# Two-layer diffusion backbone: the Fourier heads move beside attention, the context's groups move up to the latent weights, the DFT is folded twice

## The chip, the cores and the metric

One core of a Trainium2 chip runs the whole program: two layers, one launch. The metric is the device time of a run in microseconds, as the median of several runs. The shown times of the kernel before are 2538.61, 2540.79 and 2540.26 us, median 2540.26 us.

## What is computed

`x` (1024 latent tokens of width 1024) and `ctx` (256 context tokens) pass two layers; `c` and `c_ctx` give each stream its modulation vectors. Cut to what matters (all in fp32):

```
for i in 0, 1:
    sh1, sc1, g1, sh2, sc2, g2 = split(silu(c) @ ada_w[i] + ada_b[i], 6)        # the same for c_ctx
    hx = rms_norm(x) * norm1_g * (1 + sc1) + sh1;  hc likewise from ctx
    px = hx @ w_in[i]        # columns: Fourier 256, pooling 256, queries 512, keys 256, values 256
    q, k = rope(head_norm(...));  context keys and values from hc, without rope
    ax = softmax(q @ [k, kc].T / sqrt(128)) @ [v, vc]       # 4 query heads, 2 key heads, 1280 keys
    fo = real(fft2(px_fourier as 4 heads of 64, over tokens and features)) @ w_fourier[i]
    po = (windowed means - px_pool) @ w_pool[i] * pool_scale[i]
    x  = x + g1 * (concat(fo, po, ax) @ w_out[i])
    x  = x + g2 * experts(modulated norm of x)              # 16 experts, each takes its 128 tokens
    if i == 0: ctx goes the same way, attending to context keys alone
```

## The kernel before, in words

Everything is one program in Python that writes out the instructions of five engines. fp32 products are made of three fp32r products (`mm3`, line 253: high by high, low by high, high by low), so every operand is split once into a high and a low part (`split`, line 249: a ScalarE copy and a VectorE subtraction). Transposes and some small products are plain fp32.

Buffers come from rings: 43 pages of 128x1024 fp32, 8 halves (512), 4 quarters (256). A page that is taken waits for whoever used that slot last. PSUM has 8 banks; `lone` (line 1525, 1533) keeps single banks to 4 to 7 once attention begins, so that pairs are left for score rows.

The order of the work is written out with generators. `run` takes one to its end, `some(g, n)` takes n steps of it, and `interleave((g, n), ...)` takes steps of several in proportion to the numbers beside them. The scheduler that turns this into one queue per engine may move an instruction a little, but largely keeps that order. SyncE issues the plain loads, in its own order.

A layer's first half, from line 1470 on:

- The latent rows are loaded, normed and modulated (`Normed`, line 405), the Fourier columns projected (`fp_group` with weights `wf`), then the queries (`q_group`, `wq`), the pooling columns (`fp_group`, `wp`), then keys and values (`kv_group`, `wkv`), one step for each 128 tokens. A key step's norm and rope run over ScalarE, VectorE and GpSimd; `turn` transposes 512 tokens of keys at once.
- Beside the latent keys the context rows are loaded and modulated (`context_in`, line 1481). Then `fourier_w` (line 677) multiplies the Fourier weights with the DFT of the features, and the context keys follow.
- Layer 0, line 1526 on: `fourier_x` in proportion 13 to 16 with `context_groups` (line 1511), which loads 1024 columns of the input weights a second time, splits them and makes the context's queries and its Fourier and pooling columns. Then latent pooling (`pool_mix`, line 823) beside the context's Fourier heads (`fourier_c`, line 778), then the context's pooling beside the first 6 score rows.
- Layer 1: `fourier_x` beside the context keys and pooling, then pooling beside the first 6 score rows.
- Attention (line 869) has two generators: `scores`, 32 rows (4 heads x 8 tiles: 6 products of 512 columns and 3 of 256, two row maxima, two exponentials), and `values`, 80 steps (transpose four tiles of weights, split them, 3 products of 512). Line 1543: 60 value steps, 24 rows, and 24 steps of modulation: in layer 0 `ada_part` (line 308), fp32 products with two loaded pages a step; in layer 1 `ada_rows` (line 338), VectorE passes.

`fourier_x` (line 694) before: rows 1 to 511 and 1023 to 513 are added (cosine) or subtracted (sine), products with the feature DFT give U and V of 512 rows; row 512 goes on its own, with one-row products and an alternating sign; then for each of cosine and sine a 512x512 table is loaded and split in two pages, and two output blocks take 12 products of 512 columns each. Four PSUM banks are held until sums and differences give tokens 0 to 511 and 1023 to 513.

```
    DVE.tensor_tensor(out=e[:, 1:512], in0=F[b][:, 1:512], in1=F[b][:, 1023:512:-1],
                      op=OP.subtract if z else OP.add)
```

## Time and profile before

| | |
|---|---|
| median of 3 runs | 2540.26 us (2538.61 to 2540.79) |
| the profiled execution, time | 2545.91 us |
| its span, first to last instruction | 2544.0 us |
| mean granted TensorE clock | 0.981 |
| layer 0: projections / mixed stage / first score rows / rest of attention | 57.0 to 185.2 / 259.7 / 283.5 / 444.0 us |
| layer 1: mixed stage / first score rows / rest of attention | 1592.0 to 1634.8 / 1659.8 / 1808.0 us |

A view by windows gives, for each stretch, how long each engine was busy in it; a view of groups gives the mean duration of one kind of instruction; a view of waits says which engine a queue waited for. All instructions carry line 107, that of the helper that issues them, so a stage is known by the names of its tiles: `pg`, `hf`, `qt` are pages, halves and quarters, `banks` is PSUM, `cs` the constants with the identity (transposes), `altr` the alternating sign, `cond` the condition vector, `mx` the row maxima. The stages' borders in the table are the first products of each kind.

### The profile page before, as it was taken

To read this page: it belongs to the slowest core of one execution; us is meant where nothing else is said; L and a number is where in the kernel's file an instruction comes from. 1 tells how busy PE (TensorE), PEld (TensorE's weight loads), DVE (VectorE), ACT (ScalarE), POOL (GpSimd) and SP (SyncE) were. 2 spreads that over 40 slices of the span, in tenths; PEclk is the share of its full clock that TensorE was granted. 3 is DMA by queue.
4 is the path that set the end of the run, shared out by engine and by line. 5 is a ranking of instruction groups with operands and counts; after the bars stand their busy time and mean duration, and the time that the engine had idled before them with its cause. 6 is when DMAs were issued, how large, how long until landed. Compare 5 with 4: busy or idle time off the path is not lost. (4 is left out here: it accounts for less than half of the span.)

```text
span 2544.0 us, 39662 instructions
## 1 busy us (share of the span) xinstructions
PE 2425.6 (95%) x14709; PEld 1843.9 (72%) x14709; DVE 1930.5 (76%) x3114; ACT 1384.2 (54%) x1934; POOL 324.5 (13%) x350
## 2 busy tenths in 40 slices
PE   7999999999899999999999899899995999999998
PEld 4878667775677777777777687678774778888886
DVE  4547756756988787787777675887746999999997
ACT  4124546422555656666666412466523777787775
POOL 1320000001111011121010252100000111011100
PEclk9999999999999999999999999999997999999999
DMA  7113341547798889899887642210566999999993
GB/s 288 51 33 111 108 133 36 182 143 265 274 285 295 280 281 304 286 289 301 290 291 249 201 149 71 63 42 1 199 223 224 355 345 364 390 382 386 383 398 98
DMA packets 175075, 575.51 MB, mean 226 GB/s; under 512 B 22361, under 2 KB 35065, under 8 KB 174881
## 3 DMA queue, kind: packets, MB, share of 16 engines
q1 hardware_dynamic: 162784, 535.22, 59.0%
q0 software_dynamic: 12096, 37.75, 6.3%
q8 instruction: 115, 1.88, 0.3%
q14 instruction: 80, 0.65, 0.1%
HBM read 535.10 MB, written 37.80 MB: 225 GB/s over the span
## 5 line engine op out<-in xcount | busy, mean ns | idle before, releaser
L107 PE MATMUL banks<-pg,pg 128*128 128x512 f32 (+2 forms) x9656 | 1982.2, 393 | 18.4 <-DVE pg L107 9.9
L107 PEld LDWEIGHTS banks<-pg,pg 128*128 128x128 f32 (+1 forms) x9656 | 1448.4, 172 | 397.1 <-issue 29.8
L107 ACT ACTIVATE pg<-pg 128x1024 fp32r<-128x1024 f32 (+3 forms) x945 | 931.8, 1008 | 550.8 <-PE banks L107 354.3
L107 DVE TENSOR_TENSOR pg<-pg,pg 128x1024 fp32r<-128x1024 f32 (+3 forms) x918 | 1040.9, 1158 | 194.6 <-ACT pg L107 181.6
L107 ACT ACTIVATE pg<-banks 128x512 fp32r<-128x512 f32 (+3 forms) x438 | 243.6, 581 | 242.6 <-PE banks L107 231.3
L107 DVE TENSOR_TENSOR pg<-banks,pg 128x512 fp32r<-128x512 f32 (+2 forms) x404 | 257.6, 662 | 69.0 <-ACT pg L107 64.4
L107 PE MATMUL banks<-cs,pg 128*128 128x128 f32 x1616 | 243.2, 282 | 41.3 <-DVE pg L107 31.5
L107 PEld LDWEIGHTS banks<-cs,pg 128*128 128x128 f32 x1616 | 196.6, 145 | 95.0 <-DVE pg L107 44.6
L107 ACT ACTIVATE hf<-banks 128x512 f32<-128x512 f32 (+3 forms) x126 | 66.4, 541 | 245.9 <-PE banks L107 230.6
L107 PE MATMUL banks<-pg,hf 128*128 128x512 f32 (+1 forms) x660 | 165.2, 371 | 13.8 <-ACT pg L107 6.6
L107 PEld LDWEIGHTS banks<-pg,hf 128*128 128x128 f32 x660 | 113.8, 196 | 48.5 <-ACT pg L107 10.9
L107 DVE TENSOR_REDUCE mx<-banks 128x1 f32<-128x256 f32 (+1 forms) x136 | 106.4, 795 | 33.2 <-PE banks L107 32.4
L107 ACT ACTIVATE pg<-banks,nb 128x256 f32<-128x256 f32 (+1 forms) x136 | 104.2, 773 | 43.4 <-DVE nb L107 40.5
L107 POOL TENSOR_SCALAR rnv<-ss 128x1 f32<-128x1 f32 x38 | 17.5, 461 | 673.6 <-ACT pg L107 610.1
L107 POOL DMA_INDIRECT pg<-xtab,idxx x32 | 45.2, 1414 | 420.9 <-PE banks L107 137.5
L107 POOL DMA_INDIRECT xmid<-pg,idxx x16 | 37.0, 2311 | 448.4 <-DVE pg L107 448.4
L107 DVE TENSOR_TENSOR hf<-banks,pg 128x512 f32<-128x512 f32 x36 | 24.8, 690 | 67.4 <-PE banks L107 67.2
L107 POOL DMA_INDIRECT out_dram<-pg,idxx x16 | 39.7, 2484 | 243.9 <-DVE pg L107 116.1
L107 DVE TENSOR_TENSOR pg<-pg,hf 128x512 f32<-128x512 f32 (+1 forms) x68 | 42.5, 627 | 24.5 <-POOL hf L107 23.5
L107 PE MATMUL banks<-pg,qt 128*32 128x256 f32 x1024 | 58.6, 381 | 0.5 <-ACT qt L107 0.5
L107 PE MATMUL banks<-pg,cond 128*32 128x512 f32 x256 | 56.0, 618 | 2.1 <-DMA pg<-in_ada_w_dram 2.1
L107 PEld LDWEIGHTS banks<-pg,qt 128*32 128x32 f32 x1024 | 31.6, 110 | 25.4 <-issue 2.9
(148 smaller groups left out, 1071.5 us busy)
## 6 DMA issues: line engine op xcount, KB each, us to landing
pg<-in_w_gate_dram SPq DMA_DIRECT2D x256, 512.0 KB
pg<-in_w_up_dram SPq DMA_DIRECT2D x256, 512.0 KB
pg<-in_w_down_dram SPq DMA_DIRECT2D x256, 512.0 KB
pg<-in_ada_w_dram SPq DMA_DIRECT2D x96, 512.0 KB
pg<-in_w_in_dram SPq DMA_DIRECT2D x32, 512.0 KB
pg<-in_x_dram SPq DMA_DIRECT2D x16, 512.0 KB
pg<-in_w_out_dram SPq DMA_DIRECT2D x16, 512.0 KB
xtab<-pg SPq DMA_DIRECT2D x16, 512.0 KB
```

Source lines behind the costliest of these rows:

```text
L107: r = fn(*a, **k)
```

## The change

- `fourier_x` folds the rows a second time, about row 256, into even and odd output tokens; a table becomes one page for each parity (256 columns), row 256 and row 0 or 512 change their places, and the sum for token 512 comes out of the same bank. One bank is held at a time. Even and odd tokens are written with a stride of two.
- In layer 0 the context's loads and modulation start beside the last Fourier columns of the latents, and the context's groups are made with `wf`, `wq` and `wp` as these are in place; `context_groups` and its loads go.
- In layer 0 the context keys come before the latent keys, and latent pooling runs beside the last four latent key steps. In layer 1 two of the four pooling steps run beside the context keys.
- Attention comes straight after. One queue of side work, `beside`, holds what is left: (layer 1: two pooling steps), `fourier_x`, then in layer 0 `fourier_c`, the context's pooling and the two `ada_part`, in layer 1 `ada_rows`. 4 of its steps go beside the first 6 score rows, up to 36 beside the next 60 value steps.

```diff
-    dl = np.stack(dft(T, 512, 512, 1.0 / 256))
+    cl, sl = dft(T, 256, 512, 1.0 / 256)
+    dl = np.stack([np.stack([a[:, par::2] for a in (cl, sl)]) for par in range(2)])
...
-    alt512 = altr[:, None, :].to_broadcast([1, 256, 2])
+    alt256 = altr[:, None, :].to_broadcast([1, 128, 2])
...
+    DVE.scalar_tensor_tensor(altm, iota, 0.0, cs[:, 429:430].to_broadcast([128, 128]), op0=OP.is_equal, op1=OP.mult)
...
-            kb = page()
+            kb = page() if big else half()
...
     def fourier_x(F, pcw, oT):
...
-                e = half()
...
+                e, g = page(), half()
                 DVE.tensor_tensor(out=e[:, 1:512], in0=F[b][:, 1:512], in1=F[b][:, 1023:512:-1],
                                   op=OP.subtract if z else OP.add)
...
+                if z == 0:
+                    DVE.tensor_copy(e[:, 0:513:512], F[b][:, 0:513:512])
+                    split(mid(128 * b, 128 * b + 128), e[:, 256:257].to_broadcast([128, 128]))
...
+                for par in range(2):
+                    DVE.tensor_tensor(out=g[:, 256 * par:256 * par + 256], in0=e[:, 0:256], in1=e[:, 512:256:-1],
+                                      op=OP.add if z == par else OP.subtract)
+                split(fold(512 * b, 512 * b + 512), g.ap)
+                drop(e, g)
+                yield
...
-        pq = []
-        for z in range(2):
-            tab = Weights(dl[z], 512, 4)
-            run(tab.load())
+        for par in range(2):
+            raw, tab = page(), Pair(page)
+            SP.dma_start(raw.ap, dl[par])
+            split(tab(0, 1024), raw.ap)
+            drop(raw)
             for m in range(2):
...
+                for n in range(2):
+                    mm3(p, uv(0, n), tab(256 * n, 256 * n + 256), n == 0, par == 1 and n == 1)
+                if par == 0:
+                    v = p.rearrange("p (a b) -> p a b", b=2)
+                    PE.matmul(v, um[0], alt256, start=False, stop=False)
+                    PE.matmul(v, um[1], alt256, start=False, stop=True)
+                for n in range(2):
+                    mm3(q, uv(1, n), tab(512 + 256 * n, 768 + 256 * n), n == 0, par == 1 and n == 1)
+                if par == 0:
+                    for n in range(2):
+                        for part in uv(0, n):
+                            PE.matmul(q[:, 0:128], part, altm, start=False, stop=False)
+                    PE.matmul(q[:, 0:128], um[0], altm[0:1, :], start=False, stop=False)
+                    PE.matmul(q[:, 0:128], um[1], altm[0:1, :], start=False, stop=True)
                 yield
+                qs = quarter()
+                ACT.activation(qs.ap, q, AF.Copy)
+                x, y = oT(m, 0, 512), oT(m, 512, 512)
...
+                    DVE.tensor_sub(x[:, 1:512:2], p, qs.ap)
+                    DVE.tensor_add(y[:, 511:0:-2], p, qs.ap)
+                drop(qs, ps)
...
-        interleave((fx_steps, 2), (some(rows_of, 3), 3))
-        drop(wf)
+        interleave((fx_steps, 2), (some(rows_of, 3), 3) if last else (some(ci, 2), 2))
...
+        if last:
+            drop(wf)
+            interleave((qx, 8), (wp.load(), 4), (some(rows_of, 12), 12))
+        else:
+            interleave((some(qx, 3), 3), (ci, 7))
...
+            run(fp_group(C, hc, wf, FC[0:2]))
+            drop(wf)
+            interleave((qx, 5), (wp.load(), 4))
+            run(q_group(C, hc, wq, qtab[2], QC))
...
         interleave((fp_group(X, hx, wp, FX[2:4]), 4), (wkv.load(), 4), (some(rows_of, 9), 9))
+        if not last:
+            run(fp_group(C, hc, wp, FC[2:4]))
...
+        if last:
+            interleave((some(kvx, 9), 9), (later(ci, 10), 20))
...
+            run(some(kvc, 1))
+            run(kvx)
+            px = pool_x()
+            interleave((kvc, 3), (some(px, 2), 2))
+        else:
...
+            run(some(kvc, 3))
+            run(some(kvx, 1))
+            run(kvc)
+            run(some(kvx, 4))
+            interleave((some(kvx, 4), 4), (pool_x(), 4))
...
+        cw = fourier_w(i)
+        run(kvx)
         sx, vx = attention(X, Q, kx, kc, oX)
...
+        def beside():
+            yield from px
+            yield from fourier_x(FX[0:2], cw, oX)
+            if last:
...
+                yield from rows_of
+                return
+            yield from fourier_c(FC[0:2], cw, oC)
+            yield from pool_mix(C, FC[2:4], pw, oC)
...
+            yield from ada_part(0, 1)
+            yield from ada_part(0, 2)
+        side = beside()
+        interleave((some(sx, 6), 6), (some(side, 4), 4))
...
-        interleave((some(vx, 60), 60), (some(sx, 24), 24), *side)
+        interleave((some(vx, 60), 60), (some(sx, 24), 24), (side, 36))
```

## Rows read from the trace of the kernel before

**Rows 1.** Page, part 1: busy us, share of the span, instructions.

```profile
PE 2425.6 (95%) x14709; PEld 1843.9 (72%) x14709; DVE 1930.5 (76%) x3114; ACT 1384.2 (54%) x1934; POOL 324.5 (13%) x350
```

**Rows 2.** Windows of layer 0: length, busy us by engine, granted clock, DMA share, GB/s.

```profile
57.00:185.20 128.20, 126.00 (x550) 102.33 (x549) 61.24 (x112) 28.43 (x50) 41.26 (x65) 0.99 0.14 42
185.20:259.70 74.50, 69.19 (x438) 60.47 (x436) 60.08 (x119) 35.59 (x63) 8.18 (x25) 0.98 0.34 102
259.70:283.50 23.80, 20.14 (x88) 15.86 (x89) 18.33 (x53) 14.09 (x31) 0.00 (x0) 0.86 0.21 67
283.50:444.00 160.50, 160.33 (x877) 108.89 (x876) 101.75 (x210) 87.89 (x188) 0.00 (x0) 0.99 0.31 100
```

**Rows 3.** Windows of layer 1, the same columns.

```profile
1592.00:1634.80 42.80, 40.50 (x199) 31.54 (x197) 38.42 (x83) 19.43 (x38) 5.35 (x14) 0.96 0.21 61
1634.80:1659.80 25.00, 19.31 (x84) 14.16 (x84) 21.05 (x43) 14.35 (x31) 0.00 (x0) 0.93 0.16 48
1659.80:1808.00 148.20, 146.41 (x844) 118.85 (x843) 121.08 (x242) 104.33 (x216) 0.00 (x0) 1.00 0.16 52
```

**Rows 4.** Waits of TensorE, layer 0, 185.2 to 283.5 us: total us, times, longest.

```profile
PE banks L107 <- DVE hf L107: 5.6, 3, 3.2
```

**Rows 5.** Waits of TensorE, layer 1, 1592 to 1659.8 us.

```profile
PE banks L107 <- DVE pg L107: 2.3, 1, 2.3
```

**Rows 6.** Timeline of TensorE, layer 0: start us, us, instructions merged.

```profile
179.44 5.76 PE L107 MATMUL banks<-pg,pg 128*128 128x512 f32 x24
...
213.16 0.38 PE L107 MATMUL banks<-qt,altr 1*128 1x256 f32 x1
213.47 1.44 PE L107 MATMUL banks<-pg,pg 128*128 128x256 f32 x10
...
232.87 11.69 PE L107 MATMUL banks<-pg,pg 128*128 128x512 f32 x97
```

**Rows 7.** Groups by shape, 185.2 to 259.7 us: count, busy us, mean ns, idle before.

```profile
L107 DVE TENSOR_TENSOR pg<-pg,pg 128x1024 fp32r<-128x1024 f32 x13 | 15.7, 1217 | 5.2 <-ACT pg L107 3.9 <-PE banks L107 1.3
...
L107 DVE SCALAR_TENSOR_TENSOR hf<-pg,cs,pg 64x512 f32<-64x512 f32 x8 | 6.0, 748 | 0.3
...
L107 DVE TENSOR_TENSOR pg<-banks,pg 128x512 fp32r<-128x512 f32 x8 | 5.4, 680 | 0.0
...
L107 DVE TENSOR_TENSOR pg<-pg 64x512 f32<-64x512 f32 x4 | 2.8, 688 | 0.1
...
L107 DVE TENSOR_TENSOR pg<-pg 128x527 f32<-128x527 f32 x4 | 2.7, 700 | 0.0
...
L107 DVE TENSOR_TENSOR pe<-pg,cs 64x8 f32<-64x8 f32 x10 | 1.5, 158 | 0.1
```

**Rows 8.** The same on VectorE, 1592 to 1659.8 us.

```profile
L107 DVE TENSOR_REDUCE mx<-banks 128x1 f32<-128x1024 f32 x8 | 9.7, 1215 | 2.9 <-PE banks L107 2.9
...
L107 DVE SCALAR_TENSOR_TENSOR pg<-pg,cond,pg 128x1024 f32<-128x1024 f32 x3 | 3.8, 1279 | 0.0
...
L107 DVE TENSOR_REDUCE mx<-banks 128x1 f32<-128x256 f32 x6 | 2.5, 416 | 0.5 <-PE banks L107 0.5
...
L107 DVE TENSOR_TENSOR pg<-banks,pg 128x256 fp32r<-128x256 f32 x5 | 2.0, 418 | 0.0
...
L107 DVE TENSOR_SCALAR nb<-mx 128x1 f32<-128x1 f32 x6 | 1.2, 202 | 0.0
...
L107 DVE TENSOR_TENSOR tot<-sums 128x1 f32<-128x1 f32 x5 | 0.8, 156 | 0.4 <-ACT pg L107 0.2
...
L107 DVE TENSOR_TENSOR hf<-pg,hf 128x128 fp32r<-128x128 f32 x2 | 0.6, 284 | 0.0
```

**Rows 9.** DMA issues, 185.2 to 259.7 us: queue, count, KB each.

```profile
pg<-in_w_in_dram SPq DMA_DIRECT2D x8, 512.0 KB
```

**Rows 10.** Timeline of TensorE, modulation products (cond), layer 0.

```profile
285.63 1.06 PE L107 MATMUL banks<-pg,cond 128*32 128x512 f32 x8
...
300.70 1.04 PE L107 MATMUL banks<-pg,cond 128*32 128x512 f32 x2
```

More of the change, by code (lines that the diff above doesn't have):

```diff
@@ L696, in fourier_x @@
         UV = []
+        midb = half(F32R)
+        mid = lambda a, b: (midb[:, a:b], midb[:, 256 + a:256 + b])
         for z in range(2):
@@ L723, in fourier_x @@
         ps = bank()
-        midb = half(F32R)
-        mid = lambda a, b: (midb[:, a:b], midb[:, 256 + a:256 + b])
-        for b in range(2):
-            split(mid(128 * b, 128 * b + 128), F[b][:, 512:513].to_broadcast([128, 128]))
         for b in range(2):
@@ L767, in fourier_x @@
         drop(umid, *UV)
-        for m in range(2):
-            qs = half()
-            ACT.activation(qs.ap, pq[2 + m].ap, AF.Copy)
-            DVE.tensor_sub(oT(m, 0, 512), pq[m].ap, qs.ap)
-            y = oT(m, 512, 512)
-            DVE.tensor_add(y[:, 511:0:-1], pq[m][:, 1:512], qs[:, 1:512])
-            DVE.tensor_copy(y[:, 0:1], y512[:, m:m + 1])
-            drop(qs, pq[m], pq[2 + m])
-            yield
     def fourier_c(F, pcw, oT):
         cw = lambda z, b: pcw(512 * z + 256 * b, 512 * z + 256 * b + 256)
-        fs = Pair(half)
+        fs, uvs = Pair(page), Pair(page)
@@ L1467, in backbone @@
         fx_steps = fp_group(X, hx, wf, FX[0:2])
-        interleave((some(fx_steps, 2), 2), (hx.modulate(1), 10), *side)
-        interleave((fx_steps, 2), (some(rows_of, 3), 3))
-        drop(wf)
-        qtab = rope_tables(i, q_norm_g, "q")
-        Q = []
-        interleave((q_group(X, hx, wq, qtab, Q), 8), (wp.load(), 4), (some(rows_of, 12), 12))
-        drop(wq, *qtab[:2])
-        FX += [page() for _ in range(2)]
-        ktab = rope_tables(i, k_norm_g, "k")
-        interleave((fp_group(X, hx, wp, FX[2:4]), 4), (wkv.load(), 4), (some(rows_of, 9), 9))
-        drop(wp)
-        kx = KV(X)
         def context_in():
```

122 lines of the change are left out of this document (43 added, 79 removed).

## The prediction

> **What bounds the kernel now.** I read the page first: TensorE is busy 95% of the span, VectorE 76% [rows 1]. Most of that is expert work that the change leaves alone, so I read only the stretches in which each layer goes from its projections to the end of the latent attention, in windows cut where the work changes: 57 to 444 us in layer 0 [rows 2], 1592 to 1808 us in layer 1 [rows 3]. In each, the same stages stand behind each other. The projections are TensorE's (126.00 of 128.20 us busy, VectorE 61.24). Then comes a mixed stage: context keys, Fourier heads, pooling, in layer 0 the context's other groups too. Here VectorE is the full engine (60.08 of 74.50, and 38.42 of 42.80 in layer 1), and TensorE waits for it [rows 4, 5]. The first score rows, up to the first value product, stay on VectorE (18.33 of 23.80, 21.05 of 25.00), with the granted clock at 0.86 and 0.93. After that attention is TensorE's: 160.33 of 160.50 and 146.41 of 148.20 busy, at 0.99 and 1.00. A move therefore helps only if it takes VectorE work out of the middle; TensorE work that it puts beside attention is paid in full.
>
> **Prices of one instruction.** 97 products of 256 columns take 11.69 us and 24 of 512 take 5.76 us [rows 6]: without the last one's tail, 0.119 and 0.232 us each. A product with one row as the weights holds TensorE for 0.31 us (from 213.16 to 213.47 us). On VectorE a pass over 1024 columns takes 1.22 us, over 512 0.68 [rows 7], over 256 0.42, over 128 0.28 [rows 8].
>
> **The folded DFT, per layer.** Before: 62 products of 256 columns, 48 of 512, 6 of one row: 7.4+11.1+1.9 = 20.4 us of TensorE. After, read from the diff: 48 for U and V, 6 for the middle row and 48 for the two tables, all of 256 columns, 102 x 0.119 = 12.1; 8 of one row 2.5; 8 with 128 moving columns. No row has that form: half of 0.119 bounds it from below, the 512-column price from above, 0.5 to 1.9 us; I take 0.119, the nearest, 1.0. Sum 15.6, so 4.8 us less. On VectorE each of the four folds gains two 256-column passes (4 x 0.84), and two of four table splits go (2.4): about 1 us more.
>
> The trace halves the time with the columns. The Trainium skill ("TensorE: Matmul & The Clock Gate", Back-to-back issue gap) gives another sustained spacing, 81 ns at 128 columns and 131 ns at 512, so that the columns hardly count; by that, with an estimate of 98 ns at 256 columns, the products other than the one-row ones would save 1.7 us a layer where rows 6 say 5.4. The measured 0.232 us is far from its 131 ns, so the sum goes by the rows.
>
> **Layer 0, context groups with the latent weights.** Eight loads of 512 KB [rows 9] and their eight splits go, 8 x 1.22 us of VectorE, all out of the mixed stage. The query group's 96 products of 256 become 48 of 512: 11.4 to 11.1 us. The context's loads, modulation, query and Fourier and pooling groups move up among the projections, where VectorE is half idle. On SyncE's queue its two loads now pass the rope tables and the pooling weights; the DMA engines are 14% busy in that stretch, so this costs nothing unless the pages are late. On GpSimd the norms of two query tiles come into a queue busy 41.26 of 128.20. The first Fourier weights stay until the context has used them, and I count all 43 pages in use when the latent keys begin, so a page can be late: from 0 to 4.6 us, twice the nearest wait for one page, 2.3 [rows 5]; I take 2. The last latent key step, before at 185.2 us, then ends at 185.2+11.1 (queries)+11.4 (Fourier, pooling)+11.1 (context keys)+0.4 (their transposes)+2 = 221.2 us.
>
> From there VectorE sets the pace, for pooling now lies beside the last latent key steps. Its passes are 8 over the full width of 0.70, 4 of 0.69, 8 of 0.75 and 16 small ones of 0.16 [rows 7]: 17.0 us. Four key steps of five 256-column passes (8.4) and two splits of transposed keys (1.4) make it 26.8, in 4 x 24 x 0.232 = 22.3 us of TensorE's; 4.5 are left over. Behind them stand the last key step 2.1, the Fourier weights 1.4, the last key splits 1.4 and the first query split 0.7: the first score comes 10.1 us later, at 231.3. Six score rows of 2.16 (a maximum over 1024 columns, one over 256, three small ones [rows 8]) are 13.0, two query splits 1.4, the two cosine folds 5.3, two splits of U 1.4: 21.1, so the first value product comes at 252.4, before at 283.5. The rest of attention is TensorE's 160.5 plus what is put beside it: the Fourier products left 12.7, the context's DFT 48 x 0.119 = 5.7, its pooling 0.9; 2 more for changes between kinds of work.
>
> **Modulation, beside what is left.** The 18 steps that make the modulation rows stand behind Fourier in one queue of side work and get about the second half of the first 60 value steps, where they had three quarters. A step takes TensorE 1.06 us; one that comes apart because its second page is late takes 1.04+1.06 [rows 10]. Of the 16 with loads I count 8 apart now; from -8 to +8 us, I take +2. The end is 252.4+160.5+19.3+4 = 436.2 us against 444: **7.8 us less.**
>
> **Layer 1.** No context groups, the same order. From the last key step at 1592.0 VectorE has its rest 2.5, two context key chains 3.4, half the pooling 7.1 and splits of keys, Fourier weights and query 4.3: 17.3 us, TensorE about 16; the first score comes at 1609.3, before at 1634.8. Then six rows and their query splits 14.4, the other half of pooling 9.9, two folds 5.3: 29.6, the first value at 1638.9, before at 1659.8. Then 148.2+15.6+1.5 = 165.3: 1804.2 against 1808, **3.8 us less.** The three modulation passes of 1.28 us that sat among the first score rows [rows 8] go into the middle, where VectorE has 27 us free.
>
> **Sum.** 11.6 us less, if VectorE never pauses in those four stretches (10.1+21.1+17.3+29.6 = 78.1 us). In layer 1's mixed stage it was busy 90%, and waits of its own chain remain, though pooling and folds fill most: I allow 3. That leaves 8.6 us. The profiled execution took 2545.9 us (span 2544.0 and 1.9 around it), 5.6 over the median of 2540.3; by the sum it becomes 2537, and the median **2532 us**. A measurement of this kernel tells about 0.2%, 5 us, from no change.
>
> **Rivals.**
> - *Stalls get filled.* Up to the first value product I left TensorE idle about 6+7 us in layer 0 and 1+16 in layer 1. If Fourier products and the first transposes are placed there, two thirds, 20 us, come back: **2512**. For: beside attention TensorE's queue already mixes five kinds of work with no idle time. Against: each of them waits for a split on the same full VectorE.
> - *The gain is given back.* All eight whole modulation steps come apart, and TensorE pays 6 us beyond the 2 in the sum: **2538**, no change that could be told. For: twice the load rate, with a ring of pages that is nearly full. Against: the DMA share there is only 0.31.
> - *The change doesn't do what it says:* the folded products don't run at half price, and only the reordering is left. The 4.8 us a layer are gone: **2541**. The row of 97 products speaks against it. By the spacing of the Trainium skill ("TensorE: Matmul & The Clock Gate", Back-to-back issue gap) 3.7 us a layer would be gone, 2539.
> - *Slower: VectorE's queue pauses in front of the scores.* What covered its latencies in the mixed stage, Fourier's product chains, now lies behind; pooling and folds stand in its queue ahead of the row maxima, for which every score waits. If it is busy there only as among the first score rows now, 0.8 in the mean [rows 2, 3], the 78.1 us become 97.6, 16.5 more than with my allowance: **2548**. It decides from 90 us on, a share of 0.87, where the whole 11.6 us are gone. For: those rows are the same work. Against: there VectorE lacked work; now it has a backlog.
>
> **How the numbers follow.** The forecast has 0.40 (own range 2521 to 2542: 0.33 faster, 0.07 same), filled stalls 0.24, gain given back 0.10 and unfolded price 0.04 (together 0.01 faster, 0.12 same, 0.01 slower), the pausing queue 0.22, all slower. Faster 0.58, same 0.19, slower 0.23. The range runs from 2506, the filled stalls with the low ends of the unknown costs, to 2551, the pausing queue with late pages.
>
> **What the next profile would show.** Right: one-row and 256-column products lie inside attention; the first value product comes some 31 us earlier in layer 0 and 20 in layer 1; the rest of attention is longer by 23 and 17 us; eight loads of the input weights are gone; VectorE is over 90% busy from the pooling to the first value. Wrong: if the stretch from the last key step to the first value exceeds 31 us in layer 0 or 47 in layer 1 with VectorE idle in it, the queue pauses; if the rest of attention grows by less than the added products, stalls were filled; if layer 0's last key step ends later than 221 us, pages were late. A change in the experts' stages would be outside all of this.

## The result, and the profile after

Four runs of the changed kernel have a median of 2525.35 us (2524.4 to 2526.89), four of the kernel before 2540.53 us (2538.61 to 2545.41). The ratio is 0.9934 with a 95% interval of 0.9919 to 0.9949: 15.2 us faster, which is clear of the 0.2% that can be told from no change, inside the forecast's range and 6.7 us below its 2532.

The first line of the page of the changed kernel answers to [rows 1]: TensorE has 15.8 us less to do, VectorE 7.8, and the span, 2522.4 us, is 21.6 shorter than the one the prediction was made from.

```profile
PE 2409.8 (96%) x14665; PEld 1830.0 (73%) x14665; DVE 1922.7 (76%) x3124; ACT 1374.4 (54%) x1924; POOL 326.6 (13%) x346
```

The windows of layer 0 in the changed kernel answer to [rows 2]; the columns are the same, and the cuts are again the last latent key step, the first score, the first value product and the end of attention.

```profile
57.00:221.20 164.20, 161.77 (x754) 131.96 (x753) 83.20 (x155) 37.22 (x70) 49.72 (x73) 1.00 0.11 33
221.20:234.60 13.40, 7.30 (x24) 4.51 (x23) 10.81 (x26) 4.85 (x11) 4.36 (x7) 0.75 0.00 0
234.60:257.80 23.20, 19.65 (x106) 16.61 (x107) 20.89 (x48) 15.78 (x36) 0.00 (x0) 0.93 0.00 1
257.80:437.30 179.50, 177.92 (x1029) 126.10 (x1027) 118.61 (x263) 98.25 (x208) 0.60 (x5) 1.00 0.34 110
```

The mixed stage of 74.5 us has become 13.4. Most of its TensorE work now stands in the first window, 161.77 busy of 164.20 us, and in the last, 177.92 of 179.50. Attention ends at 437.3 us; before it was 444.0.

The windows of layer 1 in the changed kernel, answering to [rows 3], with one more row ahead of them, the latent key steps (before: 1534.7 to 1592.0 us):

```profile
1523.20:1574.20 51.00, 47.10 (x215) 38.07 (x214) 31.77 (x63) 15.10 (x33) 16.95 (x34) 1.00 0.22 71
1574.20:1598.20 24.00, 18.50 (x81) 14.16 (x79) 21.07 (x49) 8.56 (x17) 5.07 (x10) 0.93 0.07 17
1598.20:1623.50 25.30, 21.60 (x90) 15.62 (x89) 21.91 (x56) 15.81 (x36) 0.00 (x0) 0.87 0.00 0
1623.50:1787.50 164.00, 162.22 (x959) 132.81 (x958) 138.59 (x274) 112.87 (x228) 1.26 (x2) 1.00 0.20 64
```

The last three windows make 213.3 us, before 216.0. And the key steps, which the prediction left as they were, take 51.0 us where they took 57.3.

TensorE's waits in the changed kernel, layer 0, 221.2 to 257.8 us (total us, times, longest), answering to [rows 4]:

```profile
PE banks L111 <- DVE hf L111: 5.6, 1, 5.6
PE banks L111 <- ACT pg L111: 3.4, 2, 3.2
```

The same view of layer 1, 1574.2 to 1623.5 us, answering to [rows 5]:

```profile
PE banks L111 <- DVE pg L111: 3.6, 2, 2.9
PE banks L111 <- DVE hf L111: 3.4, 2, 2.6
PE banks L111 <- ACT pg L111: 2.2, 3, 1.6
```

VectorE is still what TensorE waits for most between keys and values: 5.6 of 9.5 us in layer 0, all of it for the last pooling step's half (hf), and 7.0 of 9.2 in layer 1. TensorE's timeline in the middle of layer 0's attention answers to [rows 6]:

```profile
285.02 0.97 PE L111 MATMUL banks<-pg,pg 128*128 128x256 f32 x6
285.92 0.48 PE L111 MATMUL banks<-altr,qt 1*128 1x256 f32 x2
286.34 0.98 PE L111 MATMUL banks<-pg,pg 128*128 128x256 f32 x6
287.15 0.56 PE L111 MATMUL banks<-altm,pg 128*128 128x128 f32 x4
287.64 0.43 PE L111 MATMUL banks<-altm,qt 1*128 1x128 f32 x2
```

These are the folded Fourier products, inside attention as the change says. The new form, four products of 128 columns, takes 0.49 us to the next one's start, 0.12 each in the mean. Last, the DMA issues of the changed kernel from 57 to 257.8 us, answering to [rows 9]: the input weights are loaded six times in all that time, and not once behind 185.2 us, where eight loads stood.

```profile
pg<-in_w_in_dram SPq DMA_DIRECT2D x6, 512.0 KB
```

### The profile page after: what moved, and what is told of

Its sections match the earlier page's. It is cut to its first block, busy times and chain, and to the rows that moved or that the text cites. A ratio compares the mean times of both kernels' runs of the same rounds, so it can differ in the third digit from the quotient of the medians.

```text
span 2522.4 us, 39523 instructions
## 1 busy us (share of the span) xinstructions
PE 2409.8 (96%) x14665; PEld 1830.0 (73%) x14665; DVE 1922.7 (76%) x3124; ACT 1374.4 (54%) x1924; POOL 326.6 (13%) x346
## 5 line engine op out<-in xcount | busy, mean ns | idle before, releaser
L111 ACT ACTIVATE pg<-pg 128x1024 fp32r<-128x1024 f32 (+3 forms) x935 | 921.1, 1007 | 527.4 <-PE banks L111 350.5
L111 DVE TENSOR_TENSOR pg<-pg,pg 128x1024 fp32r<-128x1024 f32 (+2 forms) x908 | 1027.5, 1157 | 185.1 <-ACT pg L111 172.9
L111 ACT ACTIVATE pg<-banks 128x512 fp32r<-128x512 f32 (+4 forms) x440 | 245.2, 581 | 258.6 <-PE banks L111 246.2
L111 PE MATMUL banks<-cs,pg 128*128 128x128 f32 x1608 | 239.5, 279 | 37.8 <-DVE pg L111 27.6
L111 PEld LDWEIGHTS banks<-cs,pg 128*128 128x128 f32 x1608 | 190.8, 143 | 92.6 <-DVE pg L111 42.5
L111 PE MATMUL banks<-pg,hf 128*128 128x512 f32 (+1 forms) x612 | 153.5, 373 | 7.0 <-ACT pg L111 5.6
L111 PEld LDWEIGHTS banks<-pg,hf 128*128 128x128 f32 x612 | 105.9, 194 | 35.4 <-ACT pg L111 8.7
L111 DVE TENSOR_REDUCE mx<-banks 128x1 f32<-128x1024 f32 (+1 forms) x136 | 105.7, 795 | 24.0 <-PE banks L111 23.1
L111 POOL TENSOR_SCALAR rnv<-ss 128x1 f32<-128x1 f32 x38 | 21.1, 555 | 525.8 <-ACT pg L111 458.4
```

The costliest lines, as they stand in the source:

```text
L111: r = fn(*a, **k)
```

## The experiments

Twelve runs were made, three of them of unchanged kernels. The theory was the prediction's: the gain is VectorE work taken out of the middle, and cheaper Fourier products. The rivals were that the fold alone does it, that the place of the Fourier heads does it, or that a stage outside the two attentions does it. The table has what the traces of all of them show, cut at the starts of products in TensorE's timeline: the end of layer 0's attention (the first product of its output projection), the expert stage of layer 0, which no kernel changes, then in layer 1 the latent key steps (from the first of their 192 products to the last), the stretch from that last product to the first of the output projection (an earlier cut than the end of the windows above), and the span. All in us.

| kernel | layer 0's attention ends | experts | key steps, layer 1 | last key to output, layer 1 | span |
|---|---|---|---|---|---|
| before | 444.6 | 785.6 | 57.1 | 200.1 | 2544.0 |
| c_before (unchanged) | 444.6 | 787.8 | 55.2 | 199.9 | 2542.5 |
| e_fold | 439.7 | 783.2 | 54.1 | 201.8 | 2533.1 |
| e_unfold | 439.1 | 786.5 | 51.5 | 203.0 | 2533.6 |
| e_front | 434.4 | 787.7 | 52.6 | 198.4 | 2526.2 |
| after | 437.3 | 783.6 | 50.6 | 197.2 | 2522.4 |
| c_after (unchanged) | 438.1 | 783.1 | 52.5 | 196.6 | 2524.4 |
| a_same (unchanged) | 438.1 | 785.7 | 51.9 | 196.9 | 2526.6 |
| e_hyb | 434.4 | 786.3 | 52.9 | 196.8 | 2524.0 |
| e_ktab | 437.6 | 783.2 | 53.2 | 196.7 | 2525.1 |
| e_rows | 439.3 | 786.2 | 53.3 | 197.9 | 2530.2 |
| e_pool | 435.6 | 783.4 | 53.3 | 198.8 | 2525.7 |
| b1 | 433.4 | 783.8 | 52.8 | 196.5 | 2521.0 |
| b3 | 434.1 | 783.8 | 64.4 | 189.8 | 2524.6 |

The experts take 783.1 to 787.8 us, and the changed kernel alone has 783.1, 783.6 and 785.7: two spans may differ by some 4 us that no edit made. So the parts are compared stage by stage, and only where they differ by more than unchanged kernels do. Of the 21.6 us between the first and the sixth row's spans, the four columns hold 7.3, 2.0, 6.5 and 2.9; the other 2.9 are spread over the rest of the kernel.

### Both kernels once more

The unchanged kernels, each with a second profile, to see how far a stage repeats.

> The kernel before, unchanged, for a second profile. In the first one TensorE stood 4.2 us in layer 1's latent key steps for a late load of key weights and then ran 7 us at the low clock; with it the key steps took 57.3 us, in the changed kernel 51.0. Theory (an accident of that one execution): the key steps take 50 to 52 us here and the span is 2536 to 2540. Rival (the order of the loads makes the stall, and the change removed it): 56 to 58 us again, and a span of 2543 to 2546.

> The changed kernel, unchanged, for a second profile. Outside the two stretches that the change rewrites, the first profile of it was some 5 us shorter than that of the kernel before (2 in layer 0's experts, 1.5 at the start of layer 1, 1.9 elsewhere). Theory (these differences are execution noise or small shifts of TensorE's clock): they come out otherwise here, by a microsecond or more each. Rival (they belong to the change): the same stages agree within 0.5 us with the first profile.

The kernel before took 2544.36 us (span 2542.5), the changed one 2526.46 (span 2524.4). The end of layer 0's attention repeats within 0.8 us, and so does layer 1's stretch behind the keys. The experts took 783.1 us in c_after, as its rival had it (783.6 in the first profile), but 785.7 in a_same below. Of the stages that the change touches, the key steps of layer 1 vary most: 57.1 and 55.2 before, 50.6 and 52.5 after. The windows of these steps, first in the kernel before:

```profile
1534.70:1592.00 57.30, 50.96 (x213) 40.66 (x212) 29.54 (x60) 14.34 (x31) 16.64 (x33) 0.91 0.20 70
```

The same steps of c_before:

```profile
1535.30:1590.80 55.50, 50.55 (x214) 40.20 (x213) 28.95 (x60) 13.66 (x30) 16.64 (x33) 0.94 0.21 71
```

And of c_after:

```profile
1524.10:1577.00 52.90, 49.88 (x214) 40.39 (x213) 31.85 (x63) 15.21 (x33) 16.94 (x34) 0.94 0.20 69
```

So the length before was no accident of one profile, though c_before lies between its theory's 50 to 52 us and its rival's 56 to 58. A part of the differences is the clock: the same products keep TensorE busy for 50.96 us at 0.91, 50.55 and 49.88 at 0.94, and 47.10 at 1.00 (the changed kernel's row above).

### The fold alone, and everything but the fold

e_fold is the kernel before with the new Fourier function and its tables in the old places (the function itself, as in the change, is left out here):

```diff
-            interleave((fx, 13), (chain(some(context_groups_, 4), kvc, context_groups_), 16))
+            interleave((fx, 15), (chain(some(context_groups_, 4), kvc, context_groups_), 16))
...
-            interleave((fx, 11), (chain(kvc, some(px, 3)), 4))
+            interleave((fx, 13), (chain(kvc, some(px, 3)), 4))
...
-            drop(*FX[0:2])
```

> The kernel before with the twice-folded DFT alone, in the old order. Theory (the mixed stage belongs to VectorE, so TensorE time saved in it is worth nothing there): 2540 plus or minus 3, with TensorE's Fourier products at 15 to 16 us a layer instead of 20 to 25. Rival (the saving of 4.8 us a layer is had wherever it lies): 2531.

e_front is the changed kernel with the Fourier heads of the latents ahead of attention again, so it has the fold and the context groups with the latent weights, but not the Fourier heads beside attention:

```diff
+        run(fourier_x(FX[0:2], cw, oX))
         sx, vx = attention(X, Q, kx, kc, oX)
...
-            yield from fourier_x(FX[0:2], cw, oX)
```

> The changed kernel with the Fourier heads put back in front of attention, one after the other, all else as changed. Theory (placing them beside attention only trades VectorE time in front for TensorE time beside): some 13 us a layer more in front of the first score, 13 to 16 us a layer less behind, so 2525 plus or minus 5, with a few us lost to latencies: 2522 to 2532. Rival (the placement is where the gain comes from): 2538 or more.

e_unfold is e_front with the old Fourier function and tables (left out here too):

```diff
         run(fourier_x(FX[0:2], cw, oX))
+        drop(*FX[0:2])
         sx, vx = attention(X, Q, kx, kc, oX)
```

> The kernel with the Fourier heads in front of attention (the run that had them there in both layers, 2529.8 us, layer 0's attention to 434.4 us), but with the DFT folded once as in the kernel before: order and context groups alone. In the old order the second fold alone brought layer 0's attention end from 444.6 to 439.7 us and layer 1 nothing. Theory (the fold is worth the same in either order, for the Fourier heads are a serial chain in layer 0 both times): layer 0's attention ends at 439 to 440 us, layer 1 within 2 us, 2532 to 2536. Rival (without the second set of weights VectorE has room in front, and the fold is worth nothing): 434 to 435 us, 2528 to 2531.

Measured: e_fold 2536.18 us, ratio 0.9985 (0.9975 to 0.9995); e_unfold 2534.99, 0.9981 (0.9970 to 0.9993); e_front 2529.83, 0.9961 (0.9947 to 0.9974). e_fold lies between its theory (2537 to 2543) and its rival (2531), the other two inside their theories. In layer 0 the two parts are two sides of a square: the fold alone ends attention 4.9 us earlier (444.6 to 439.7), the order without the fold 5.5 (439.1), both 10.2 (434.4). They add up. The changed kernel, whose Fourier heads lie beside attention, ends at 437.3 to 438.1: that place alone costs 2.9 to 3.7 us of layer 0. In layer 1 it gives some back: from the first key step to the output projection e_front takes 251.0 us, the changed kernel 247.8 to 249.1. For the two layers together the new place of the Fourier heads is about neutral, and that rival falls.

In layer 1 the fold alone gave nothing behind the keys, 201.8 us from the last key step to the output against 200.1. In the new order it did: e_front takes 198.4 us there and e_unfold 203.0, where the expectation had the two within 2 us. So in layer 1 the parts don't simply add up, and why is open. The window of e_fold that answers to the first of [rows 3] shows what became of the saving in the old order:

```profile
1579.90:1625.50 45.60, 39.49 (x200) 33.51 (x199) 39.52 (x94) 17.62 (x38) 5.09 (x13) 0.85 0.09 26
```

VectorE has 39.52 us to do where it had 38.42; TensorE has products of half the columns to run, stands idle for longer (6.1 us instead of 2.3), and is busy 39.49 us instead of 40.50, at a granted clock of 0.85 instead of 0.96. What was taken from TensorE's work came back as waiting and as the lower clock. In layer 0 the same fold in the same place did give time: the mixed stage of e_fold, 184.8 to 256.6 us,

```profile
184.80:256.60 71.80, 66.08 (x444) 58.41 (x442) 61.07 (x137) 34.85 (x64) 8.79 (x25) 0.98 0.31 93
```

has TensorE 92% busy, at 0.98, and became 2.7 us shorter than in [rows 2]. There TensorE was the fuller engine before the change too, 69.19 of 74.50 us against VectorE's 60.08.

The three windows of e_front, layer 0:

```profile
220.80:257.30 36.50, 28.44 (x151) 23.26 (x149) 27.52 (x64) 15.41 (x31) 4.79 (x12) 0.81 0.10 34
257.30:278.40 21.10, 19.86 (x123) 17.35 (x123) 17.94 (x48) 14.19 (x33) 0.31 (x1) 1.00 0.34 103
278.40:434.40 156.00, 155.56 (x886) 108.86 (x886) 105.67 (x225) 90.10 (x191) 0.00 (x0) 1.00 0.31 103
```

In the first, neither engine is full: 28.44 and 27.52 of 36.50 us, at a granted clock of 0.81. TensorE waits once for 5.6 us for pooling there, as in the changed kernel, and runs the Fourier products behind that wait. Beside attention they run at 1.00 with no idle time, but are paid in full: the last stage of the changed kernel is 23.5 us longer than this one (179.50 to 156.00) and what is before it 20.6 shorter (278.4 to 257.8). That is the 2.9 us.

### The key steps of layer 1

In the changed kernel the key tables are made behind the pooling weights' release. e_ktab puts them ahead again in layer 1:

```diff
+        if last:
+            ktab = rope_tables(i, k_norm_g, "k")
         interleave((fp_group(X, hx, wp, FX[2:4]), 4), (wkv.load(), 4), (some(rows_of, 9), 9))
...
-        ktab = rope_tables(i, k_norm_g, "k")
+        if not last:
+            ktab = rope_tables(i, k_norm_g, "k")
```

> The changed kernel, but in layer 1 the rope tables of the keys are loaded ahead of the key weights again, as in the kernel before. Theory (the change shortened layer 1's key steps because the two table loads no longer stand ahead of the key weights on SyncE's queue and take no pages there): the last load of key weights is issued after the first key step begins, the key steps take 54 to 57 us where the changed kernel has 50.6 and 52.5, and the time is 2528 to 2531. Rival (that difference is chance): 50 to 53 us, 2525.

Measured: 2527.5 us, 0.9946 (0.9933 to 0.9959), key steps 53.2 us: short of the theory's 54 to 57 and just above the rival's 50 to 53. What lies under them is the fourth load of key weights. Its issue on SyncE's queue in the kernel before (start us, us; the key steps begin at 1534.7):

```profile
1535.59 0.38 SPq L107 DMA_DIRECT2D pg<-in_w_in_dram  x1
```

In the changed kernel, where they begin at 1523.2:

```profile
1521.19 0.38 SPq L111 DMA_DIRECT2D pg<-in_w_in_dram  x1
```

In e_ktab, where they begin at 1522.8:

```profile
1523.09 0.38 SPq L111 DMA_DIRECT2D pg<-in_w_in_dram  x1
```

0.9 us behind the first key step, 2.0 ahead of it, and 0.3 behind it. The waits of TensorE in the key steps follow. The kernel before:

```profile
PE banks L107 <- ACT pg L107: 4.2, 1, 4.2
PE banks L107 <- DVE pg L107: 2.1, 1, 2.1
```

The changed kernel:

```profile
PE banks L111 <- DVE pg L111: 3.9, 2, 3.5
```

And e_ktab:

```profile
PE banks L111 <- ACT pg L111: 2.7, 1, 2.7
PE banks L111 <- DVE pg L111: 1.8, 1, 1.8
```

The wait for ScalarE's half of the weights' split is there in the first and the third and gone in the second: the order of the loads makes it. But e_ktab's key steps lie inside the 50.6 to 53.3 us of the kernels in the new order (b3 aside, which puts other work among them), because the later wait on VectorE is 2.1 us shorter there. So the late load explains one wait and about 1 us net, not the whole difference. e_unfold has 51.5 us without the fold and e_fold 54.1 with it, so the fold isn't needed for the gain.

The rest can be read from TensorE's idle time and clock. Idle it was 6.3 and 5.0 us in the two profiles of the kernel before, and 3.9, 3.0 and 3.5 in the three of the changed one: 2.2 us less in the mean. What remains of the 4.5 us by which the key steps differ in the mean is the lower clock of the rows above, and that is partly chance of an execution. In the changed kernel's first profile TensorE waits 3.5 us in these steps and goes on at full speed:

```profile
1555.50 1.20 PE L111 MATMUL banks<-cs,pg 128*128 128x128 f32 x9 [3.53 <-DVE pg L111]
1556.45 5.78 PE L111 MATMUL banks<-pg,pg 128*128 128x512 f32 x24
```

In c_after the same kernel waits 3.0 us at the same place, and the same products behind it take 2.8 us longer, up to the next transposes:

```profile
1555.55 2.18 PE L111 MATMUL banks<-cs,pg 128*128 128x128 f32 x9 [3.02 <-DVE pg L111]
1557.38 7.70 PE L111 MATMUL banks<-pg,pg 128*128 128x512 f32 x24
```

Why the clock fell in the one and not in the other stays open.

### The first score rows

e_rows takes the side work away from beside the first six score rows:

```diff
-        interleave((some(sx, 6), 6), (some(side, 4), 4))
+        run(some(sx, 6))
...
-        interleave((some(vx, 60), 60), (some(sx, 24), 24), (side, 36))
+        interleave((some(vx, 60), 60), (some(sx, 24), 24), (side, 40))
```

> The changed kernel without any side work beside the first six score rows; its 4 steps move behind them. Theory (VectorE's queue paces the first score rows, so folds and pooling in it delay them): first score to first value 16 to 18 us in layer 0 and 16 to 20 in layer 1 instead of 23.2 and 25.3, the rest of attention 3 and 2 us longer, 2516 to 2520 in all. Rival (the rows wait for their own chain of score, maximum and exponential, and VectorE had room): 21 to 24 us in both, the rest longer by the same 3 and 2, 2528 to 2531.

e_pool moves pooling the other way, behind the keys altogether:

```diff
-            interleave((kvc, 3), (some(px, 2), 2))
+            run(kvc)
...
-            interleave((some(kvx, 4), 4), (pool_x(), 4))
-            px = iter(())
+            run(some(kvx, 4))
+            px = pool_x()
```

> The changed kernel with all latent pooling in the queue of side work, so that its four steps lie beside the first six score rows in both layers and the folds behind. Theory (VectorE time in front of the scores counts in full, and pooling only changes its place within it): last key step to first score 8 us in layer 0 instead of 13.9 and 18 in layer 1 instead of 24.4; first score to first value some 10 us longer in layer 0 and 2 in layer 1; 2523 to 2529. Rival (pooling in front delays the scores, beside them it finds room): both stretches together 6 us a layer shorter, 2511 to 2516.

Measured: e_rows 2532.09 us, 0.9968 (0.9956 to 0.9980); e_pool 2527.77, 0.9942 (0.9929 to 0.9955). The first score rows of layer 0 and the rest of attention in e_rows:

```profile
236.10:257.20 21.10, 17.23 (x82) 13.79 (x83) 16.33 (x39) 13.61 (x30) 0.00 (x0) 0.92 0.00 2
257.20:439.30 182.10, 180.68 (x1051) 129.75 (x1050) 123.78 (x273) 100.19 (x212) 0.59 (x5) 1.00 0.34 109
```

VectorE has 4.6 us less to do among the six rows (16.33 against 20.89), and they get only 2.1 us shorter, as the rival had it. No engine is full in what is left (TensorE 17.23, VectorE 16.33, ScalarE 13.61 of 21.10 us), so some 21 us seems to be what the rows need by themselves: row maximum, exponentials, transposes, one behind the other. More than half of what VectorE did beside them was free, and so the side work was in the right place: without it attention ends at 439.3, later, not earlier. (Of the 7.8 us between this span and the changed kernel's, 5.3 lie in the experts and in layer 1's key steps, where the edit changes nothing in the program.) In layer 1 pooling's steps got in among the rows all the same (VectorE 21.25 of 24.30 us), so there the run says nothing.

In e_pool the stretch from the last key step to the first score and the first score rows of layer 0 are

```profile
218.30:223.40 5.10, 3.23 (x20) 2.67 (x18) 4.92 (x13) 2.56 (x6) 0.09 (x1) 1.00 0.00 0
223.40:259.20 35.80, 26.65 (x97) 17.63 (x98) 30.87 (x73) 17.08 (x37) 1.67 (x4) 0.81 0.00 1
```

Without pooling ahead of it the first score comes 5.1 us behind the last key step, not 13.4, and that step 2.9 us earlier (218.3 to 221.2). With four pooling steps among the first score rows these take 35.8 us, VectorE 30.87 of them. These rows fit the longer of two: their own 21 us, or what VectorE has to do in them, at 0.86 to 0.90 busy.

In layer 1 the same edit gave nothing. The stretch from the last key step to the first score in e_pool:

```profile
1574.30:1599.40 25.10, 19.05 (x84) 13.90 (x82) 21.61 (x48) 9.41 (x20) 4.12 (x11) 0.87 0.02 6
```

It takes 25.1 us against 24.0, and VectorE is as busy as before, 21.61 against 21.07 us. It is much the same work: the scheduler drew pooling forward into the stretch again. Of pooling's eight passes of one form that layer 1 has, five lie in it:

```profile
L111 DVE SCALAR_TENSOR_TENSOR hf<-pg,cs,pg 64x512 f32<-64x512 f32 x5 | 3.7, 745 | 0.1
```

In the changed kernel, whose program has only four of them there, it is six:

```profile
L111 DVE SCALAR_TENSOR_TENSOR hf<-pg,cs,pg 64x512 f32<-64x512 f32 x6 | 4.5, 746 | 0.2
```

So in layer 1 e_pool hardly tested its theory (18 us there). That the first score waits for the last context key is in the changed kernel's trace: TensorE stands 2.62 us for VectorE's last pass on that key, transposes it, and goes on to the score at 1598.24 us.

```profile
1597.98 0.61 PE L111 MATMUL banks<-cs,hf 128*128 128x128 f32 x2 [2.62 <-DVE hf L111]
```

Whether this chain or VectorE's sum, 21.07 of 24.0 us, sets the length isn't told apart by that.

### Three other orders

e_hyb takes the better place of the Fourier heads in each layer: e_front's edit in layer 0 alone.

```diff
+        if not last:
+            run(fourier_x(FX[0:2], cw, oX))
         sx, vx = attention(X, Q, kx, kc, oX)
...
-            yield from fourier_x(FX[0:2], cw, oX)
+            if last:
+                yield from fourier_x(FX[0:2], cw, oX)
```

> The changed kernel with the Fourier heads in front of attention in layer 0 alone. With them in front in both layers, layer 0 ended its attention at 434.4 us where the changed kernel had 437.3 and 438.1, and layer 1 took 1.5 us longer. Theory (in layer 0 the context's Fourier products then fill the stalls of the first score rows, worth 3 us; in layer 1 there is nothing like them): layer 0's attention ends at 434 to 435, layer 1 as in the changed kernel, 2521 to 2524. Rival (the 3 us are chance): 2525 to 2527.

b1 adds to that e_pool's edit in layer 0 and puts all latent pooling there behind the context's Fourier heads:

```diff
             if last:
+                yield from px
+                yield from fourier_x(FX[0:2], cw, oX)
                 yield from rows_of
...
             yield from fourier_c(FC[0:2], cw, oC)
+            yield from px
             yield from pool_mix(C, FC[2:4], pw, oC)
```

> The changed kernel with two things altered in layer 0: the Fourier heads come in front of attention, and the latent pooling goes behind the context's Fourier heads in the queue of side work. Without pooling beside the key steps the last key came 2.5 us and the first score 11 us earlier; with Fourier in front the first value came at once with 5 us of context products for nothing. Theory (both hold together, for pooling's VectorE time then lies where TensorE is the bound): layer 0's attention ends at 427 to 430 us where the changed kernel has 437.3, the time is 2515 to 2519. Rival (in front the Fourier chain then waits for itself as it did for pooling, and the rest pays for pooling): 434 to 436, 2523 to 2526.

b3 is b1 with the context keys of layer 1 moved in among the latent key steps, and layer 1's pooling behind its Fourier heads:

```diff
-            interleave((some(kvx, 9), 9), (later(ci, 10), 20))
+            run(some(kvx, 5))
+            interleave((some(kvx, 2), 2), (ci, 8))
...
-            run(some(kvc, 1))
-            run(kvx)
+            run(some(kvc, 3))
+            run(some(kvx, 1))
+            run(kvc)
+            run(some(kvx, 1))
             px = pool_x()
-            interleave((kvc, 3), (some(px, 2), 2))
```

> As b1, and in layer 1 the context is loaded and modulated beside the sixth and seventh key step, its keys come before the last key step, and pooling goes behind the Fourier heads. Theory (in layer 1 the stretch from the last key step to the first score is a chain of waits beside 11.4 us of context keys, not VectorE time): last key step to first score 6 to 10 us instead of 24.4, the key steps 11 to 13 us longer, the rest 4 longer: 2 to 6 us less than b1 in layer 1. Rival (the stretch is as long with the keys moved, since the last key's own chain and the pages make it): no gain or a loss against b1.

a_same is the changed kernel once more, beside these two on one chip.

> The changed kernel once more, timed on the chip of b1 and b3 so that they are compared with it directly: 0.9934 to 0.9950 of the kernel before, 2524 to 2528 us; layer 0's experts at one of the two levels seen so far, 783 or 786 to 788 us.

Measured: e_hyb 2526.12 us, 0.9938 (0.9925 to 0.9950). Its layer 0 is e_front's (434.4), its layer 1 the changed kernel's (196.8), as it should be by the stages; the 3 us between them are less than the spread of the experts, and the medians don't tell it from its neighbours. a_same 2526.7 us, 0.9935 (0.9921 to 0.9948); b1 2522.03, 0.9916 (0.9903 to 0.9930), the lowest of all, between its theory (2515 to 2519) and its rival (2523 to 2526); b3 2527.29, 0.9940 (0.9927 to 0.9954), 5.3 us above b1 where the theory had 2 to 6 below. b1 is surely faster than the kernel before. Against the changed kernel, 4.7 us on the same chip, the two intervals overlap; of the times themselves, four of b1's five lie below all five of a_same. So that it is faster is likely and not shown.

Layer 0 of b1, from the last key step on:

```profile
217.90:231.60 13.70, 10.35 (x66) 8.48 (x64) 13.20 (x33) 8.83 (x18) 1.99 (x5) 1.00 0.16 51
231.60:264.20 32.60, 32.01 (x203) 27.35 (x203) 27.29 (x63) 19.61 (x43) 0.52 (x3) 1.00 0.08 19
264.20:433.40 169.20, 162.22 (x895) 110.43 (x893) 119.88 (x264) 94.14 (x198) 0.48 (x6) 0.99 0.33 107
```

The first two are as full as could be wished. But in the last, TensorE is idle for 7.0 of 169.2 us; in the changed kernel it was 1.6 of 179.5. Layer 1 of b3:

```profile
1583.90:1588.90 5.00, 3.91 (x24) 3.05 (x22) 4.61 (x15) 3.20 (x8) 1.30 (x3) 1.00 0.00 0
1588.90:1612.60 23.70, 19.35 (x108) 15.36 (x108) 22.22 (x52) 16.15 (x36) 0.69 (x2) 1.00 0.00 1
1612.60:1773.70 161.10, 152.64 (x853) 120.68 (x851) 134.11 (x278) 100.15 (x209) 1.69 (x6) 0.98 0.14 44
```

With the context keys done early and pooling behind the Fourier heads the first score comes 5.0 us behind the last key step. The edit takes both out of the stretch, so it doesn't tell which of them made its length. The key steps, which they now lie among, are 11 to 14 us longer for it. And the rest, which ends here at the output projection, is 13.5 us longer than in a_same:

```profile
1627.00:1774.60 147.60, 145.72 (x865) 119.53 (x864) 123.85 (x253) 98.92 (x204) 1.26 (x2) 1.00 0.16 48
```

VectorE has 10.3 us more to do and TensorE 6.9, but TensorE is idle for 8.5 us instead of 1.9. Its waits in that window of b3:

```profile
PE banks L111 <- ACT pg L111: 3.6, 6, 1.0
PE banks L111 <- DVE hf L111: 3.3, 2, 2.9
```

Pooling inside attention costs TensorE idle time, though VectorE is busy for only 134 of 161 us; Fourier inside attention cost its products and hardly more. One possible reason is that pooling's long passes stand in VectorE's queue in one piece ahead of the splits that the value products need. That wasn't tried, and the waits don't bear it out by themselves: in b1 5.0 of the 6.7 us in this stretch are for ScalarE, in b3 3.6 of 7.9.

## Why the prediction was right, and where it was off

The kernel became faster by the likeliest case, and the gain was underestimated by 6.7 us. That its terms came within a microsecond or so of each layer's attention is in part luck, since errors of up to 7 us cancel. Point by point:

- **The folded products.** 15.6 us of TensorE a layer were predicted. Added up over the timeline, the Fourier products of the latents take 15.3 us in layer 0 and 15.5 in layer 1. 128 columns were taken at 0.119 us and measured 0.12; the one-row products were priced too high, 0.21 us at 256 columns and 0.18 at 128 where [rows 6] had 0.31. The rival that the products don't run at half price is out: e_fold is faster than before, and its layer 0 by 4.9 us. The Trainium skill ("TensorE: Matmul & The Clock Gate", Back-to-back issue gap) gives a sustained spacing of 81 ns for products of 128 columns and 131 for 512; no row here shows either, the nearest being 0.12 and 0.232 us.
- **What bounds the mixed stage.** The prediction calls VectorE the full engine there. Its own rows have TensorE the busier one, 69.19 of 74.50 us against 60.08 in layer 0 and 40.50 of 42.80 against 38.42 in layer 1 [rows 2, 3], so VectorE alone didn't set the pace. With TensorE's work cut, e_fold ended layer 0's attention 4.9 us earlier, and gave nothing in layer 1.
- **Layer 0.** The last key step was predicted to end at 221.2 us, and it did (its last product starts at 220.8), but not by its terms. TensorE is busy 35.8 us more up to there, where 34.0 were counted: pooling's own products, 2.0 us, stood in no term. TensorE waits 2.4 us in all, before 2.2, so no late page shows, and the 2 us held for one were free to cover it. From there: to the first score 10.1 predicted, 13.4 measured; first rows 21.1 and 23.2; rest 183.8 and 179.5. End 436.2 and 437.3. The stretch to the first score was mis-sized because VectorE's sum was taken for its length: VectorE has 10.81 us in it, near the predicted 10.1, but stands still for the rest, and TensorE waits 5.6 us for pooling. The first rows: the predicted 21.1 was also VectorE's sum (20.89 measured), and came out longer by its pauses. The end is right because these errors, +3.3 and +2.1, nearly cancel the -4.3 of the rest.
- **The rest of layer 0** was 4.3 us shorter than the forecast. The modulation steps had been taken to cost 2 us more through late pages; added up over the timeline they take 26.8 us in 25 pieces, before 27.6 in 28. That term had the wrong sign and is 2.8 of the 4.3. The rival built on it (gain given back) falls with it.
- **Layer 1.** To the first score 17.3 predicted, 24.0 measured; first rows 29.6 and 25.3; rest 165.3 and 164.0. The sum is 212.2 and 213.3, so the errors cancel. The prediction counted half of pooling ahead of the first score, and VectorE did three of its four steps there: it has 21.07 us of work in that stretch instead of 17.3, and pauses for 2.9. The first rows are shorter for the same reason, VectorE having 21.91 us in them instead of 29.6.
- **The rival that VectorE pauses** was half right. Its four stretches were to be 78.1 us, 81.1 with the allowance, and 97.6 by the rival. They are 13.4 + 23.2 + 24.0 + 25.3 = 85.9, with VectorE busy for 74.7 of them, 0.87, the very share at which the rival was to take the whole gain. It did not, since less work lay in them than was counted, and the ends came 4.3 and 1.3 us earlier than their terms. The sign that the prediction set for this rival did come: from the last key step to the first value it is 36.6 us in layer 0 (over 31) and 49.3 in layer 1 (over 47), with VectorE idle for 4.9 and 6.3 of them; over 90% busy it was not.
- **Filled stalls** (2512 us) didn't happen as put: TensorE is still idle 6.1 and 3.6 us in layer 0's stretches, 5.5 and 3.7 in layer 1's, 18.9 of the 30 us that the prediction had left, and the rest of attention grew by 19.0 and 15.8 us, much as the products put beside it were counted (19.3 and 15.6).
- **The sum.** By the windows, 6.7 us less in layer 0 (444.0 to 437.3) and 2.7 in layer 1 (216.0 to 213.3), 9.4 in all; forecast 11.6, and 8.6 with the allowance. Without the allowance each layer is 1.1 us off; with it the total is 0.8.
- **The step that failed** is the one that let layer 1 be "the same order": the change also moves the making of the key tables, and with it the fourth key-weight load past them on SyncE's queue. The prediction counted the loads that pass the tables in layer 0 and put no price on this one. The key steps took 50.6, 52.5 and 51.9 us in the three profiles of the changed kernel, 57.1 and 55.2 in the two of the kernel before: 4.5 us in the mean that no term held, the largest part of the 6.7 that were missing. Of these the load's wait is shown, 2.7 us in e_ktab, with about 1 net; another 1 is idle time of TensorE that the new order also took away, by a way that stays open, and the rest is the granted clock, 0.91 and 0.94 before and 1.00, 0.94 and 0.97 after, in part chance of an execution.
- "VectorE has 27 us free in the middle of layer 1" holds for three short modulation passes and for Fourier's splits, not for pooling: in b3 TensorE is idle for 8.5 us there.

Shown by runs: that fold and order add up in layer 0 (e_fold, e_unfold, e_front); that the Fourier heads' place is about neutral over both layers (e_front against the changed kernel); that the order of loads makes the wait in the key steps (e_ktab); that the first rows don't go much below 21 us when VectorE's side work leaves them (e_rows); that layer 1's stretch ahead of the scores falls from 24.0 to 5.0 us when context keys and pooling both leave it (b3). Open: how the order's 5.5 us in layer 0 divide between the context's groups, the early context keys and pooling, which e_unfold moves together; which of the two made layer 1's stretch, why the clock over the key steps differs from one execution to the next, why the fold gives time in layer 1 in the new order only, and why e_front, whose stages apart from the experts sum to the changed kernel's, was timed 4 us above it.

## What to carry to other kernels

Where VectorE sets the pace, a busy sum is a lower bound of a stretch's length, not its length: look for the chain in it (here 21 us of row maxima and exponentials) and fill up to that, no further. Before you plan by where the program puts a pass, read from the trace where the scheduler let it run: in layer 1 pooling ran in nearly the same place whether the program had it there or behind. Work that is halved on one engine needn't gain time: in the old order the same fold gave 4.9 us in one layer and nothing in the other, and TensorE's busy share (0.93 and 0.95 before) didn't tell which. When steps are reordered, list for every layer which DMA issue now stands ahead of which, on each queue: one load issued 3 us sooner, measured from the step that needs it, took a wait of 2.5 to 4.2 us away here.

## What was not expected of the hardware

- Four products of 128 moving columns take 0.12 us each in the timeline above, changes of form at both ends included, as long as one of 256: the halving from 512 (0.232) to 256 (0.119) doesn't go on there.
- A product with one row as the weights takes 0.21 us at 256 columns when two stand in a row (from 285.92 to 286.34 us), against 0.31 for the single one of [rows 6].
- The expert stage of layer 0, identical in all kernels, took from 783.1 to 787.8 us, and from 783.1 to 785.7 in three executions of one kernel. What makes the difference wasn't found.
- The granted clock is lower in most stretches in which TensorE waits for a few microseconds: 0.75 in the changed kernel's 13.4 us with a wait of 5.6, 0.81 in e_front's first window and in e_pool's second, and 1.00 in b1's windows at the same place, where TensorE is busy for 10.35 of 13.70 and 32.01 of 32.60 us. These are means: 0.75 is a stretch spent half at the lower level of 1.2 GHz and half at 2.4. It doesn't always fall: behind a wait of 3.5 us in the changed kernel's key steps it stayed at 1.00, behind one of 3.0 us in c_after it fell.
